# Two residual blocks in split fp32: the SBUF pools placed from both ends, TensorE's streamed operands low and its weights high

## The chip, the core and the metric

One NeuronCore of a Trainium2 chip runs the whole program in one launch. The metric is the device time of that launch in microseconds (us), the median of several runs; lower is better.

## What is computed

512 tokens of width 1024 go through two blocks, all in fp32. Each block is a SwiGLU feed-forward net (hidden width 2816), a mixer, and a second SwiGLU net, each with an RMS norm ahead and a residual around it:

```
h = h + 0.5 * ffn(rmsnorm(h), ffn1_w_in, ffn1_w_out)      # gate, up = x @ w_in; (silu(gate) * up) @ w_out
h = h + mixer(rmsnorm(h))                                  # block 1: retention + multiscale pool
                                                           # block 2: short conv + gated delta rule
h = h + 0.5 * ffn(rmsnorm(h), ffn2_w_in, ffn2_w_out)
return rmsnorm(h)
```

Some 203 MB of weights are read once; nearly all of the arithmetic is the matrix products.

## The kernel before

**Layout.** Activations lie transposed: 128 channels on the partitions, the 512 tokens along the free dimension. The residual is eight tiles h[k] of 128x512.

**Split products.** Full precision is had from one-pass matmuls (float32r) by splitting each operand: hi is the value rounded to what one pass takes (ScalarE), lo the rest (VectorE). `mm3` (L217 to L220) makes a product of three matmuls, each of 128x128 weights and 512 streamed columns, into one PSUM tile: wh with hi (L218), wh with lo (L219), wl with hi (L220). The first operand is loaded into the array (the *weights*), the second is *streamed* through it, four bytes for each column and partition.

**Weights.** `weights` (L208) loads one stage of 128x1024 fp32 by a DMA from SyncE into `wr` (three buffers), and splits it into `wh` and `wl` (three buffers each). All three tags lie in the pool `wts`.

**Streamed operands.** The rows of the residual, times a norm's gain, are split into sixteen tiles hi and lo of the pool `xsplit`; the first product of every net and mixer streams these. What comes after a first product is split into pools of its own that open and close with a stage: `act` (the 22 hidden rows of a net, for its second product), `att`, `ret`, `win`, `pool`, `mrg` in the first mixer, `ys` and others in the second. In the scores and in probabilities times values of the retention (pool `att`, lines L218 to L220 with the names psc and pso) both operands are such tiles; in the values themselves (L530 to L532) the roles are turned: the rows of `xsplit` are the weights, and `wh` and `wl` are streamed, 256 columns at a time. A norm's sums over partitions are two matmuls (L279) with the constant tile `onesr` as weights and two tiles `t` of the pool `tmp` streamed. In the second mixer L807 does what `mm3` does elsewhere, interleaved by a table with the steps of the delta rule; L722 multiplies a small tile `wbs` (16 columns of weights) with the rows of `xsplit`.

**Where pools lie.** Pools are laid in SBUF from low addresses up, in the order in which they are opened: const, hres, xsplit, wts, tmp, rows, and then those that open and close. [...]

## Time and profile before

| | us |
|---|---|
| median of 3 runs | 2308.33 (2307.97 to 2309.64) |
| the profiled execution, span from first to last instruction | 2307.3 |
| PE busy in it | 2272.6 (98%) |
| DVE busy | 1137.0 (49%) |
| ACT busy | 810.3 (35%) |
| DMA, mean rate | 90 GB/s |

The profiled execution is told by its span; the median of the runs stands 1.0 us above it. PE is TensorE's matmuls, PEld its weight loads, DVE VectorE, ACT ScalarE, POOL GpSimd. Matmuls are pipelined, so that the duration shown of one is longer than the time from its start to that of the next: what a matmul costs is read from the distance of starts in the timeline. L218 is line 218 of the kernel before.

### The profile page before, as it was taken

How to read it: one execution, taken by the hardware profiler on the slowest of the kernel's cores; microseconds unless marked ns; L12 is line 12 of the kernel's file. 1: busy time of each engine (PE TensorE's matmuls, PEld its weight loads, DVE VectorE, ACT ScalarE, POOL GpSimd, SP SyncE). 2: the span in 40 equal slices, each digit the busy share in tenths (PEclk: the TensorE clock that was granted, in tenths of full speed). 3: DMA queues.
4: the chain of work that ended last, by engine and by line, in shares of the span. 5: the costliest groups of instructions: out<-in, count | busy, mean ns of one | idle time of the engine just before them, and what ended most of it. 6: DMA issues, size and time to landing. Idle time of an engine off the chain costs nothing. (4 is left out here: it accounts for less than half of the span.)

```text
span 2307.3 us, 25697 instructions
## 1 busy us (share of the span) xinstructions
PE 2272.6 (98%) x10476; PEld 1863.1 (81%) x10476; DVE 1137.0 (49%) x1703; ACT 810.3 (35%) x1059; POOL 76.3 (3%) x78
## 2 busy tenths in 40 slices
PE   8999999999999999999999999999999999999998
PEld 6888888888878888888888888887777778888887
DVE  6444434665553444444336444334867655444332
ACT  5232223444432234233235332223534344233221
POOL 1000000000210000000000000000111000000000
PEclk9999999999999999999999999999999999999999
DMA  4333333222233333333333333333211123323332
GB/s 158 92 100 100 92 93 108 87 87 83 74 100 101 91 99 99 99 94 98 94 91 95 98 99 96 90 99 93 65 46 37 47 58 98 101 91 101 94 94 69
DMA packets 61190, 208.34 MB, mean 90 GB/s; under 512 B 6800, under 2 KB 9232, under 8 KB 61072
## 3 DMA queue, kind: packets, MB, share of 16 engines
q1 hardware_dynamic: 58544, 203.48, 28.9%
q10 hardware_dynamic: 2528, 3.21, 0.4%
q8 instruction: 82, 1.34, 0.2%
q14 instruction: 36, 0.29, 0.0%
HBM read 204.57 MB, written 2.10 MB: 90 GB/s over the span
## 5 line engine op out<-in xcount | busy, mean ns | idle before, releaser
L218 PE MATMUL ps<-hi,wh 128*128 128x512 f32 (+1 forms) x2774 | 1082.8, 391 | 6.4 <-ACT wh L202 6.4
L219 PE MATMUL ps<-lo,wh 128*128 128x512 f32 (+1 forms) x2774 | 1082.4, 390 | 0.8 <-DVE lo L206 0.8
L220 PE MATMUL ps<-hi,wl 128*128 128x512 f32 (+1 forms) x2774 | 1082.3, 390 | 0.6 <-DVE wl L203 0.6
L202 ACT ACTIVATE wh<-wr 128x1024 fp32r<-128x1024 f32 (+1 forms) x390 | 406.3, 1042 | 1159.6 <-PE ps L219 630.8
L203 DVE TENSOR_TENSOR wl<-wr,wh 128x1024 fp32r<-128x1024 f32 (+1 forms) x390 | 470.2, 1206 | 341.1 <-ACT wh L202 340.8
L218 PEld LDWEIGHTS ps<-hi,wh 128*128 128x128 f32 x2774 | 521.9, 188 | 119.5 <-ACT wh L202 6.4
L219 PEld LDWEIGHTS ps<-lo,wh 128*128 128x128 f32 x2774 | 521.5, 188 | 115.7 <-DVE lo L206 3.2
L220 PEld LDWEIGHTS ps<-hi,wl 128*128 128x128 f32 x2774 | 521.5, 188 | 114.9 <-DVE wl L203 2.5
L366 DVE TENSOR_TENSOR t<-ps,rb 128x512 f32<-128x512 f32 x88 | 60.7, 690 | 258.6 <-PE ps L220 258.6
L363 DVE TENSOR_TENSOR t<-ps,rb 128x512 f32<-128x512 f32 x88 | 60.8, 690 | 169.9 <-PE ps L220 169.8
L202 ACT ACTIVATE hi<-t 128x512 fp32r<-128x512 f32 x119 | 75.2, 632 | 112.2 <-DVE t L368 62.0
L807 PE MATMUL ps<-hi,wh 128*128 128x512 f32 x224 | 94.4, 422 | 0.4 <-DVE t L1001 0.4
L807 PE MATMUL ps<-hi,wl 128*128 128x512 f32 x224 | 93.3, 416 | 0.0
L807 PE MATMUL ps<-lo,wh 128*128 128x512 f32 x224 | 92.6, 413 | 0.0
L203 DVE TENSOR_TENSOR lo<-t,hi 128x512 fp32r<-128x512 f32 x119 | 83.3, 700 | 5.4 <-ACT hi L202 5.1
L368 DVE TENSOR_TENSOR t<-t,t 128x512 f32<-128x512 f32 x88 | 60.8, 691 | 8.2
L364 ACT ACTIVATE t<-t 128x512 f32<-128x512 f32 x88 | 54.2, 616 | 3.4 <-DVE t L363 3.3
L377 DVE SCALAR_TENSOR_TENSOR h<-ps,h 128x512 f32<-128x512 f32 x31 | 21.4, 691 | 64.4 <-PE ps L220 64.4
L807 PEld LDWEIGHTS ps<-hi,wh 128*128 128x128 f32 x224 | 42.9, 191 | 8.2 <-issue 1.0
L807 PEld LDWEIGHTS ps<-hi,wl 128*128 128x128 f32 x224 | 42.4, 189 | 8.3 <-issue 0.9
L807 PEld LDWEIGHTS ps<-lo,wh 128*128 128x128 f32 x224 | 43.1, 192 | 6.9 <-issue 0.2
L530 PE MATMUL pv<-wh,hi 128*128 128x256 f32 x128 | 36.3, 284 | 0.0
(292 smaller groups left out, 1362.1 us busy)
## 6 DMA issues: line engine op xcount, KB each, us to landing
wr<-in_ffn_w_in SPq DMA_DIRECT2D x176, 512.0 KB, 3.5
wr<-in_ffn_w_out SPq DMA_DIRECT2D x64, 512.0 KB, 3.6
wr<-in_w_in SPq DMA_DIRECT2D x48, 512.0 KB, 3.5
wr<-in_w_mix_in SPq DMA_DIRECT2D x28, 512.0 KB, 3.5
wr<-in_ffn_w_out SPq DMA_DIRECT2D x32, 384.0 KB, 3.1
wr<-in_w_v SPq DMA_DIRECT2D x8, 512.0 KB, 3.8
wr<-in_w_ret_up SPq DMA_DIRECT2D x8, 512.0 KB, 3.4
wr<-in_w_pool_up SPq DMA_DIRECT2D x8, 512.0 KB, 3.5
```

The costliest lines, as they stand in the source:

```text
L202: nc.scalar.activation(hi, src, AF.Copy)
L203: nc.vector.tensor_tensor(lo, src, hi.bitcast(F32), ALU.subtract)
L218: nc.tensor.matmul(ps, lh, rh, start=start, stop=False)
L219: nc.tensor.matmul(ps, lh, rl, start=False, stop=False)
L220: nc.tensor.matmul(ps, ll, rh, start=False, stop=stop)
L363: nc.vector.tensor_tensor(g, pg, rb, ALU.mult)
L364: nc.scalar.activation(g, g, AF.Silu)
L366: nc.vector.tensor_tensor(u, pu, rb, ALU.mult)
L368: nc.vector.tensor_tensor(m, g, u, ALU.mult)
L377: nc.vector.scalar_tensor_tensor(h[d], ps, 0.5, h[d], ALU.mult, ALU.add)
L530: nc.tensor.matmul(pv, xh[:, sl], wh[:, k % 4, :], start=(k == 0), stop=False)
L807: nc.tensor.matmul(ps, a[:, k, :], b, start=(k == j == 0), stop=(k == KD - 1 and j == 2))
```

## The change

Every SBUF pool is given a side. The side "right" lays a pool from the far end of SBUF down, the side "left" (the default) from address 0 up. `const`, `hres`, `wts`, `tmp` and `rows` go to the far end; `wh` and `wl` get a pool `wsplit` of their own there. `xsplit` and all pools that open and close with a stage stay on the left. The scratch area shrinks from 16384 to 1024 bytes. Comments and docstrings are blanked, and lines move by up to three.

```diff
+SCRATCH = 1024
...
-    def pool(self, ctx, name, psum=False):
-        kw = dict(space=bass.MemoryType.PSUM) if psum else {}
+    def pool(self, ctx, name, psum=False, far=False):
+
+        kw = dict(space=bass.MemoryType.PSUM) if psum else dict(side="right" if far else "left")
         return ctx.enter_context(self.tc.tile_pool(name=name, bufs=1, reuse_waits="tile", **kw))
...
-    const = K.pool(ctx, "const")
-    hp = K.pool(ctx, "hres")
+    const = K.pool(ctx, "const", far=True)
+    hp = K.pool(ctx, "hres", far=True)
     xp = K.pool(ctx, "xsplit")
-    wp = K.pool(ctx, "wts")
-    tp = K.pool(ctx, "tmp")
-    rp = K.pool(ctx, "rows")
+    wp = K.pool(ctx, "wts", far=True)
+    wsp = K.pool(ctx, "wsplit", far=True)
+    tp = K.pool(ctx, "tmp", far=True)
+    rp = K.pool(ctx, "rows", far=True)
...
-        wh = wp.tile([P, nk, m], F32R, name=nm("wh"), tag="wh", bufs=3)
-        wl = wp.tile([P, nk, m], F32R, name=nm("wl"), tag="wl", bufs=3)
+        wh = wsp.tile([P, nk, m], F32R, name=nm("wh"), tag="wh", bufs=3)
+        wl = wsp.tile([P, nk, m], F32R, name=nm("wl"), tag="wl", bufs=3)
...
-    nc = _bacc.Bacc("TRN2", target_bir_lowering=False, num_devices=1)
+    nc = _bacc.Bacc("TRN2", target_bir_lowering=False, num_devices=1, dynamic_dma_scratch_size=SCRATCH)
```

No instruction is added, removed or moved: both built programs have the same instructions, with the same waits, in the same order on every engine. What differs is where tiles lie. The table has the bytes within a partition at which they lie in the two built programs, and what is left of each start when it is divided by 64 (it is the same for every tile of a row, and for every slice of it that a matmul of 256 or 512 streamed columns takes, since these start at multiples of 512 bytes into their tile):

| tiles | before | mod 64 | after | mod 64 |
|---|---|---|---|---|
| hi, lo of `xsplit` | 34,976 to 67,743 | 32 | 1,152 to 33,919 | 0 |
| hi, lo of `act`, `att`, `ret`, `win`, `pool`, `mrg`, `ys` | 130,176 to 228,863 | 0 | 33,920 to 132,607 | 0 |
| `wh` | 80,032 to 92,319 | 32 | 174,016 to 186,303 | 0 |
| `wl` | 92,320 to 104,607 | 32 | 186,304 to 198,591 | 0 |
| `t` of `tmp` | 110,752 to 120,991 | 32 | 163,776 to 174,015 | 0 |
| `onesr` | 18,048 | 0 | 228,800 | 0 |
| `wbs` (starts 64 bytes apart) | 223,008 | 32 | 126,752 | 32 |
| h | 18,592 to 34,975 | 32 | 210,880 to 227,263 | 0 |

Matmuls of 512 streamed columns in float32r, counted in the built program before: 6048 stream `xsplit` against `wh` or `wl` (5376 by L218 to L220, 672 by L807); 2862 stream a stage's tiles against `wh` or `wl`; 48 have a stage's tiles on both sides; 22 are those of L279, 16 those of L722, 16 belong to the delta rule. Of 256 columns: 384 are the values of the retention (L530 to L532), 132 the last output row (L218 to L220, `act` against `wh` or `wl`), 48 the retention's scores and outputs.

## Rows read from the trace of the kernel before

**Rows 1.** The page: the span, the busy time of the engines, the granted clock of TensorE in 40 slices, and three of the costliest groups (busy us, mean ns of one | idle before them and what ended it); then the landing time of the largest group of loads.

```profile
span 2307.3 us, 25697 instructions
PE 2272.6 (98%) x10476; PEld 1863.1 (81%) x10476; DVE 1137.0 (49%) x1703; ACT 810.3 (35%) x1059; POOL 76.3 (3%) x78
...
PEclk9999999999999999999999999999999999999999
...
L218 PE MATMUL ps<-hi,wh 128*128 128x512 f32 (+1 forms) x2774 | 1082.8, 391 | 6.4 <-ACT wh L202 6.4
...
L202 ACT ACTIVATE wh<-wr 128x1024 fp32r<-128x1024 f32 (+1 forms) x390 | 406.3, 1042 | 1159.6 <-PE ps L219 630.8
L203 DVE TENSOR_TENSOR wl<-wr,wh 128x1024 fp32r<-128x1024 f32 (+1 forms) x390 | 470.2, 1206 | 341.1 <-ACT wh L202 340.8
...
wr<-in_ffn_w_in SPq DMA_DIRECT2D x176, 512.0 KB, 3.5
```

**Rows 2.** The waits of PE over the whole span, longest first in total (us in total, times, longest).

```profile
PE ps L218 <- ACT wh L202: 6.4, 1, 6.4
PE pg L918 <- DVE zu L928: 4.9, 2, 2.7
```

**Rows 3.** Busy time by stretch: from the start of the stretch to its end, its length, and the busy us and number of instructions of each engine, the granted clock, the DMA share and GB/s. The first stretch is the first product of the first net, the second the second product of block 2's first net.

```profile
35.20:252.20 217.00, 217.00 (x959) 179.73 (x958) 104.74 (x127) 72.71 (x89) 0.00 (x0) 1.00 0.32 96
...
1469.80:1592.80 123.00, 123.00 (x529) 99.03 (x528) 42.03 (x47) 33.05 (x39) 0.41 (x2) 1.00 0.32 92
```

**Rows 4.** Timeline of PE in the first product of a net (`xsplit` against `wh` and `wl`): start in us, duration, instruction. Between the third and the last row shown lie 21 more.

```profile
99.73 0.39 PE L218 MATMUL ps<-hi,wh 128*128 128x512 f32 x1
99.96 0.39 PE L219 MATMUL ps<-lo,wh 128*128 128x512 f32 x1
100.19 0.39 PE L220 MATMUL ps<-hi,wl 128*128 128x512 f32 x1
...
105.17 0.39 PE L218 MATMUL ps<-hi,wh 128*128 128x512 f32 x1
```

**Rows 5.** The same in the second product of a net (`act` against `wh` and `wl`), again with 21 rows between the third and the last.

```profile
1471.83 0.40 PE L218 MATMUL ps<-hi,wh 128*128 128x512 f32 x1
1472.06 0.40 PE L219 MATMUL ps<-lo,wh 128*128 128x512 f32 x1
1472.29 0.40 PE L220 MATMUL ps<-hi,wl 128*128 128x512 f32 x1
...
1477.43 0.40 PE L218 MATMUL ps<-hi,wh 128*128 128x512 f32 x1
```

**Rows 6.** Timeline of PE at the start of the retention's scores (both operands in `att`): the six matmuls of 512 columns, and the first of 384.

```profile
410.27 0.39 PE L218 MATMUL psc<-hi,hi 128*128 128x512 f32 x1
410.50 0.40 PE L219 MATMUL psc<-lo,hi 128*128 128x512 f32 x1
410.74 0.39 PE L220 MATMUL psc<-hi,lo 128*128 128x512 f32 x1
410.97 0.39 PE L218 MATMUL psc<-hi,hi 128*128 128x512 f32 x1
411.19 0.39 PE L219 MATMUL psc<-lo,hi 128*128 128x512 f32 x1
411.42 0.39 PE L220 MATMUL psc<-hi,lo 128*128 128x512 f32 x1
411.65 0.33 PE L218 MATMUL psc<-hi,hi 128*128 128x384 f32 x1
```

**Rows 7.** Timeline of PE around the two matmuls of a norm's sums (`t` against `onesr`; the two are shown as one row, x2), with `xsplit` against `wh` and `wl` before and after. Five rows are left out before the last.

```profile
439.29 0.39 PE L219 MATMUL ps<-lo,wh 128*128 128x512 f32 x1
439.51 0.40 PE L220 MATMUL ps<-hi,wl 128*128 128x512 f32 x1
439.75 0.63 PE L279 MATMUL pr<-t,onesr 128*128 128x512 f32 x2
440.22 0.40 PE L218 MATMUL ps<-hi,wh 128*128 128x512 f32 x1
...
441.60 0.39 PE L218 MATMUL ps<-hi,wh 128*128 128x512 f32 x1
```

**Rows 8.** Timeline of PE: the second and the sixteenth of the 16 matmuls of L722 (`xsplit` against the 16 columns of `wbs`), 14 apart.

```profile
1598.30 0.39 PE L722 MATMUL pba<-lo,wbs 128*16 128x512 f32 x1
...
1601.52 0.39 PE L722 MATMUL pba<-lo,wbs 128*16 128x512 f32 x1
```

**Rows 9.** Timeline of PE, matmuls of 256 columns: two of the retention's values, 9 apart.

```profile
398.99 0.28 PE L532 MATMUL pv<-wh,lo 128*128 128x256 f32 x1
...
400.07 0.28 PE L532 MATMUL pv<-wh,lo 128*128 128x256 f32 x1
```

**Rows 10.** The same for the last output row (`act` against `wh` and `wl`): two that are 15 apart.

```profile
2293.68 0.28 PE L220 MATMUL ps<-hi,wl 128*128 128x256 f32 x1
...
2295.45 0.28 PE L220 MATMUL ps<-hi,wl 128*128 128x256 f32 x1
```

**Rows 11.** The page's groups of two VectorE operations of one shape, one that writes tiles `t`, one that reads and writes h.

```profile
L366 DVE TENSOR_TENSOR t<-ps,rb 128x512 f32<-128x512 f32 x88 | 60.7, 690 | 258.6 <-PE ps L220 258.6
...
L377 DVE SCALAR_TENSOR_TENSOR h<-ps,h 128x512 f32<-128x512 f32 x31 | 21.4, 691 | 64.4 <-PE ps L220 64.4
```

## The prediction

> **What bounds the kernel now.** I read the page first, then the waits of PE, then stretches, then single matmuls. In the page [rows 1] PE is busy for 2272.6 of 2307.3 us at the full clock, DVE for 49% and ACT for 35%: TensorE is the bound. Its waits [rows 2] are small: 6.4 us for the first weights, then 4.9 us in the delta rule. In the products, which are most of the span, PE is busy without a gap [rows 3]: 217.00 of 217.00 us in a first product, 123.00 of 123.00 us in a second. A change that moves no instruction and no wait can only matter there by what one matmul costs. Durations don't tell that, since matmuls overlap; distances of starts do.

> In a first product 24 matmuls take 105.17 - 99.73 = 5.44 us, 226.7 ns each [rows 4]. In a second product, with the same shape, type, clock and weights buffers, 24 take 1477.43 - 1471.83 = 5.60 us, 233.3 ns each [rows 5]. [...] Nothing waits in either [rows 3], so this is a price inside TensorE's reading, and what differs between the two is where the streamed tile lies: `xsplit` in the one, `act` in the other.

> **Which property of the place?** Three readings are open, and the other rows choose between them.

> - *A high streamed tile is slow.* Against it: in the scores both operands are tiles of `att`, at 130,176 bytes or above, and after three matmuls the distances are 410.97 to 411.19 to 411.42 to 411.65, 0.22 to 0.23 us each [rows 6], the cheap price.
> - *Streamed tile and weights in different halves are slow.* The scores (both high) and the first products (both low) fit, and the second products (one high, one low) fit. The norm's sums do not fit well: there both distances together are 440.22 - 439.75 = 0.47 us, 0.235 each [rows 7], the dear price, with `onesr` at 18,048 and `t` at 110,752 and up. `wl` reaches to 104,607 and is still near to `xsplit`, so the border would have to lie between 104,608 and 110,752, which is neither half of anything in the table.
> - *Starts that differ modulo 64 bytes are slow.* By the table, first products have 32 and 32, scores 0 and 0: cheap. Second products have 0 streamed against 32, the norm's sums 32 against 0: dear. [...]

> I take the third. The change then makes every large pair equal: after it `xsplit`, the stage tiles, `wh`, `wl`, `t` and `onesr` all start at 0 modulo 64.

> **The sum.** Against the profiled execution's 2307.3 us:

> - Second products and their like: 2862 matmuls of 512 columns stream a stage's tiles against `wh` or `wl`. From 233.3 to 226.7 ns [rows 5, 4], 2862 x 6.67 ns = 19.1 us less. All of it lies on PE's path, since PE has no gap there [rows 3]. Would the loads hold? A stage of weights is used up in 24 matmuls, 5.44 instead of 5.60 us; its landing takes 3.5 us and its split 1.04 and 1.21 us [rows 1], three stages deep, and DVE is busy for 42.03 of 123.00 us [rows 3]. They do; were the cover gone, DVE's split of the next stage would be late first.
> - First products: 6048 matmuls, already cheap: 0.
> - The norm's sums: from 439.51 to 441.60 are nine distances [rows 7], 2.09 us where 9 x 226.7 ns make 2.04: 0.05 us of detour and return, eleven times: 0.5 us less.
> - 256 columns: the retention's values (32 against 32) take 1.08 us for 9, 120.0 ns each [rows 9]; the last output row (0 against 32) 1.77 us for 15, 118.0 ns [rows 10]. So the last row's 132 may go to 120.0 (0.3 us more), or the 384 values to 118.0 (0.8 us less). I take the first, since they then have equal starts as the values do; the bounds are -0.8 and +0.3.
> - VectorE and ScalarE: the same operations on tiles that lie elsewhere. Of one shape, VectorE takes 690 ns where it writes `t`, 691 where it works on h [rows 11], tiles 90,000 bytes apart: 0.
> - DMAs: none added or moved, the same order on SP's queue; the smaller scratch is one that no DMA here uses: 0.

> Together 19.1 + 0.5 - 0.3 = 19.3 us less, a span of 2288.0 us. The median of the runs stands 1.0 us above the span before, so I predict **2289 us**. A reading of starts is good to 0.01 us in 24 matmuls, at either price: 2862 x 0.8 ns = 2.4 us at most. With the values' 0.8 us and a run-to-run spread of 1.7 us this case reaches from 2284 to 2294.

> **What speaks against it.** [...] And the 16 matmuls of L722, 32 against 32, never settle at 226.7: 1601.52 - 1598.30 = 3.22 us for 14, 230.0 each [rows 8]. They have 16 columns of weights and not 128, which may excuse them.

> **The rivals.**

> - *Halves.* If a pair in different halves is dear, the change makes all of them so: weights lie at 174,016 and up, everything streamed against them below 132,608. The 2862 stay at 233.3, the 6048 go there: 6048 x 6.67 = 40.3 us more, **2348 us**, slower. It decides if the price hangs on the distance between weights and stream; L722, with weights at 223,008 and dearer than 226.7 [rows 8], speaks for it, the norm's sums and the odd border against it. 0.15.
> - *A finer rule of starts.* In rows 4 and 6 the starts agree modulo 512, not only 64; after the change they differ by 320 (174,016 less 1,152 is 337 x 512 + 320). If that counts, the nearest row is L722, whose starts differ by multiples of 64: 230.0 ns [rows 8] for all 8910 matmuls. 6048 x 3.3 = 20.0 us more, 2862 x 3.3 = 9.4 less: **2319 us**. For it: only L722 shows such pairs, and it doesn't settle. [...] 0.12.
> - *The streamed tile's place alone*, or its place as against weights that lie lower: the scores speak against the first, and nothing against the second, which halves don't need to be symmetrical for. The 2862 become cheap and the 6048 stay so: 19.1 us less, **2289 us** as well, for another reason. 0.10.
> - *The place does nothing*, and the second product is dearer for a reason of its own, such as its 66 matmuls into one PSUM tile as against 24: **2308 us**. Against it: the norm's sums, two matmuls into a tile, are dear as well [rows 7]. 0.08.

> [...]

> **How the numbers follow.** My case has 0.55. The bound of telling from no change is 0.2%, 4.6 us. Faster: 0.55 + 0.10 = 0.65. Same: 0.08. Slower: 0.15 + 0.12 = 0.27. The likeliest case's own range is 2284 to 2294. The range for 8 in 10 takes in the case of no effect and the finer rule with the same 2.4 us of reading, 2284 to 2322; left out are the halves.

> **What would show it.** Right: in a second product 24 matmuls in 5.44 us, a stretch of 528 matmuls in about 119.7 instead of 123.2 us, the two of a norm's sums 0.45 us apart from start to the next product, the first products still at 5.44 us, PE still without gaps. Wrong: first products at 5.60 us (halves), or at 5.5 with an uneven pattern (finer rule); or second products still at 5.60 (no effect of place). [...]

## The result

The changed kernel takes **2341.78 us** (median of 4 runs, 2340.92 to 2342.66) where the kernel before takes 2308.98 on the same chip (2307.97 to 2309.80): a ratio of 1.0142, with a 95% interval of 1.0128 to 1.0156. It is slower by 32.8 us. The prediction said 2289, with a range that ended at 2322.

In the page of the changed kernel, the answers to [rows 1]:

```profile
span 2339.1 us, 25697 instructions
PE 2305.0 (99%) x10476; PEld 1858.6 (79%) x10476; DVE 1138.0 (49%) x1703; ACT 810.1 (35%) x1059; POOL 76.0 (3%) x78
...
PEclk9999999999999999999999999999999999999999
...
L221 PE MATMUL ps<-hi,wh 128*128 128x512 f32 (+1 forms) x2774 | 1092.2, 394 | 6.4 <-ACT wh L205 6.4
...
L206 DVE TENSOR_TENSOR wl<-wr,wh 128x1024 fp32r<-128x1024 f32 (+1 forms) x390 | 470.5, 1207 | 341.4 <-ACT wh L205 341.1
```

The span grew by 31.8 us and PE's busy time by 32.4. The clock, the counts and the other engines are as before: VectorE's split of a stage takes 1207 ns (1206 before). All of the loss is in TensorE's own pace.

The stretches that answer to [rows 3], the first product of the first net and the second product of block 2's first net (it begins 25.4 us later now):

```profile
35.20:252.20 217.00, 217.00 (x932) 173.93 (x931) 102.77 (x125) 71.60 (x87) 0.00 (x0) 1.00 0.29 92
...
1495.20:1618.20 123.00, 123.00 (x529) 99.11 (x528) 42.09 (x47) 33.08 (x39) 0.41 (x2) 1.00 0.31 92
```

PE has no gap in either. In the same 217 us the first product gets through 932 matmuls instead of 959; the second product is at its 529 as before.

The timeline of PE, places that answer to [rows 4, 9, 7, 5, 10] in this order. In the first product and in the second the two rows are 24 matmuls apart; the values' two (L535) 9 apart; then the norm's sums and the next product; the last row's two 15 apart.

```profile
100.03 0.39 PE L221 MATMUL ps<-hi,wh 128*128 128x512 f32 x1
...
105.62 0.39 PE L221 MATMUL ps<-hi,wh 128*128 128x512 f32 x1
...
406.45 0.28 PE L535 MATMUL pv<-wh,lo 128*128 128x256 f32 x1
...
407.51 0.28 PE L535 MATMUL pv<-wh,lo 128*128 128x256 f32 x1
...
447.57 0.62 PE L282 MATMUL pr<-t,onesr 128*128 128x512 f32 x2
448.03 0.39 PE L221 MATMUL ps<-hi,wh 128*128 128x512 f32 x1
...
1490.25 0.40 PE L221 MATMUL ps<-hi,wh 128*128 128x512 f32 x1
...
1495.85 0.40 PE L221 MATMUL ps<-hi,wh 128*128 128x512 f32 x1
...
2325.41 0.28 PE L223 MATMUL ps<-hi,wl 128*128 128x256 f32 x1
...
2327.18 0.28 PE L223 MATMUL ps<-hi,wl 128*128 128x256 f32 x1
```

24 matmuls of a first product take 105.62 - 100.03 = 5.59 us, 233 ns each: they went from the cheap price to the dear one. 24 of a second product take 5.60 us, the dear price, as before. So nothing became cheap, and what was cheap is lost. The values became cheaper, 1.06 us for 9, 117.8 ns against 120.0. The last fifteen of the last row stay at 1.77 us, 118.0 each, but the greater part of that row became cheaper. Two of its matmuls 24 apart, in the kernel before and in the changed one:

```profile
2279.91 0.28 PE L220 MATMUL ps<-hi,wl 128*128 128x256 f32 x1
...
2282.75 0.28 PE L220 MATMUL ps<-hi,wl 128*128 128x256 f32 x1
```

```profile
2312.14 0.28 PE L223 MATMUL ps<-hi,wl 128*128 128x256 f32 x1
...
2314.86 0.28 PE L223 MATMUL ps<-hi,wl 128*128 128x256 f32 x1
```

That is 2.84 us against 2.72, 118.3 ns each against 113.3. Why the last fifteen differ from these was not traced.

The small product that answers to [rows 8], L725 now, two matmuls 14 apart again:

```profile
1623.72 0.40 PE L725 MATMUL pba<-lo,wbs 128*16 128x512 f32 x1
...
1626.93 0.39 PE L725 MATMUL pba<-lo,wbs 128*16 128x512 f32 x1
```

It takes 3.21 us, 229.3 ns each, where it took 230.0.

**Where the 31.8 us lie.** By the first starts of each stage in the two traces, the first products of the four nets went from 246.10, 239.67, 240.46 and 239.67 us to 253.00, 246.62, 247.09 and 246.62: 27.4 us. The first mixer took 4.9 us more, the second 0.1 less, the second products of the nets nothing (122.96 and 122.97 for the first net's), the tail after the last of them, with the last row, 0.5 less. Sum: 31.7.

### The profile page after: what moved, and what is told of

Its sections match the earlier page's. It is cut to its first block, busy times and chain, and to the rows that moved or that the text cites. A ratio compares the mean times of both kernels' runs of the same rounds, so it can differ in the third digit from the quotient of the medians.

```text
span 2339.1 us, 25697 instructions
## 1 busy us (share of the span) xinstructions
PE 2305.0 (99%) x10476; PEld 1858.6 (79%) x10476; DVE 1138.0 (49%) x1703; ACT 810.1 (35%) x1059; POOL 76.0 (3%) x78
## 3 DMA queue, kind: packets, MB, share of 16 engines
q10 hardware_dynamic: 2528, 3.21, 0.5%
## 5 line engine op out<-in xcount | busy, mean ns | idle before, releaser
L206 DVE TENSOR_TENSOR wl<-wr,wh 128x1024 fp32r<-128x1024 f32 (+1 forms) x390 | 470.5, 1207 | 341.4 <-ACT wh L205 341.1
```

The source lines that it names most:

```text
L206: nc.vector.tensor_tensor(lo, src, hi.bitcast(F32), ALU.subtract)
```

## The experiments

How prices are read here: a stretch counts every matmul that reaches into it, two more than it has distances. 100 us at 226.7 ns hold 441 and show x443; at 233.3 they hold 429 and show x430 or x431. One count is 0.5 ns. Below, a **difference** is the streamed tile's start less that of its weights, modulo 512 or, later, 256; counted so, the changed kernel has 1,152 - 174,016 = -338 x 512 + 192, a difference of 192 (the 320 of the prediction is the same, counted from the weights). The pads are tiles that nothing uses. Each kernel here but the last was run once. The kernel before took 2309.25 us beside the first four, 2309.62 beside the one with differences of 32 to 8, and 2309.43 beside the others.

Three readings were to be told apart first: that different *halves* are dear; that starts must be *alike modulo 512*, the finer rule; and that the place itself counts, both starts at 32 modulo 64 being cheap.

**The kernel before with every tile 32 bytes higher.**

```diff
+    const.tile([P, 8], F32, name="pad")
     vec = const.tile(...)
```

> The kernel before with a pad of 32 bytes per partition ahead of everything: all tiles move up by 32 bytes, so xsplit and the weights both start at 0 modulo 64 (192 modulo 512), and the stage tiles at 32 (160 modulo 512). Halves (streamed tile and weights on different sides of a border are dear): nothing changes, first products 226.7 ns a matmul, second products 233.3, 2309 us. Equal starts modulo 512 (dear unless streamed tile and weights start alike): the same, 2309 us, since first products still agree and second ones still differ by 32. [...]

Measured: 2309.75 us. The stretches of net 1's first product and net 3's second product:

```profile
100.00:200.00 100.00, 100.00 (x443) 82.78 (x442) 46.65 (x56) 30.54 (x37) 0.00 (x0) 1.00 0.31 96
1470.00:1570.00 100.00, 100.00 (x430) 80.48 (x430) 35.37 (x40) 27.66 (x33) 0.00 (x0) 1.00 0.31 91
```

Nothing moved: first products cheap, second products dear. First products now start at 0 modulo 64, which by the third reading makes them dear, and second products stream from 32, so the residue itself doesn't count; what counts depends on the pair.

**The kernel before with the weights 320 bytes higher.** All stays low, only the difference of first products changes, from 0 to 192.

```diff
+    wp.tile([P, 80], F32, name="pad")
     vec = const.tile(...)
```

> The kernel before with a pad of 320 bytes at the start of the weights' pool: weights and all that lies above them move up by 320 bytes, xsplit stays. Streamed tile and weights of the first products then differ by 320 modulo 512, as they do after the change, with both still in the low half. Halves: first products stay at 226.7 ns, 2309 us. Equal starts modulo 512: first products go to 233.3 ns, about 2342 us. Both at 32 modulo 64: xsplit is at 32 and the weights too (480 modulo 512), so 226.7 ns and 2309 us.

Measured: 2341.56 us, the time of the change.

```profile
100.00:200.00 100.00, 100.00 (x430) 80.17 (x429) 45.04 (x54) 29.45 (x36) 0.00 (x0) 1.00 0.30 95
1470.00:1570.00 100.00, 100.00 (x430) 80.52 (x429) 35.84 (x41) 27.01 (x32) 0.00 (x0) 1.00 0.32 92
```

All of the loss is here without any pool at the far end. The halves are refuted as its cause.

**The changed kernel with the streamed side 320 bytes higher.** The halves stay apart, the difference becomes 0.

```diff
+    xp.tile([P, 80], F32, name="pad")
     vec = const.tile(...)
```

> The changed kernel with a pad of 320 bytes ahead of xsplit: everything on the left side moves up by 320 bytes, so that xsplit, the stage tiles and the weights all start alike modulo 512 (448), with weights still in the high half and all streamed tiles in the low one. Halves: nothing changes, first and second products 233.3 ns, 2342 us. Equal starts modulo 512: both go to 226.7 ns, about 2289 us. Both at 32 modulo 64: all are at 0, so 2342 us.

Measured: 2290.0 us, span 2288.2.

```profile
100.00:200.00 100.00, 100.00 (x443) 82.77 (x442) 46.86 (x57) 30.66 (x38) 0.00 (x0) 1.00 0.30 95
1470.00:1570.00 100.00, 100.00 (x443) 82.81 (x442) 35.51 (x40) 28.77 (x35) 0.00 (x0) 1.00 0.33 98
```

320 bytes turn the change from 33 us slower than before to 19 us faster, and both products are cheap.

**The kernel before with only the stages' tiles 32 bytes higher.** The counterpart with everything low: second products get a difference of 0.

```diff
+    rp.tile([P, 8], F32, name="pad")
     vec = const.tile(...)
```

> The kernel before with a pad of 32 bytes at the start of the pool rows: the stage tiles move up by 32 bytes, xsplit and weights stay. All then start alike modulo 512 (160) and at 32 modulo 64, with the stage tiles still high and the weights low. Halves: nothing changes, second products 233.3 ns, 2309 us. Equal starts modulo 512: second products go to 226.7 ns, about 2289 us. Both at 32 modulo 64: the same, 2289 us.

Measured: 2291.12 us.

```profile
100.00:200.00 100.00, 100.00 (x443) 82.81 (x442) 46.69 (x57) 30.57 (x37) 0.00 (x0) 1.00 0.31 95
1470.00:1570.00 100.00, 100.00 (x443) 82.79 (x442) 35.51 (x40) 28.45 (x34) 0.00 (x0) 1.00 0.34 101
```

Both are cheap again. So equal starts are cheap wherever the two tiles lie; 64 is not enough to agree in, 512 is. The next two ask in what they must agree, with four differences each.

**Differences of 64, 128, 192 and 256.** The kernel just told, with a pad of its own at the start of `act` in each net.

```diff
+    act_pads = [64, 128, 192, 256]
...
             ap = K.pool(c, nm("act"))
+            ap.tile([P, act_pads.pop(0) // 4], F32, name=nm("pad"))
```

> Stage tiles start at 160 modulo 512 as xsplit, wh and wl do, but the pool act of the four nets begins 64, 128, 192 and 256 bytes later in turn, so that the second products of the four nets (528, 528, 528 and 462 matmuls of 512 columns) have starts that differ by 64, 128, 192 and 256 modulo 512. All else has equal starts. The same kernel without these pads took 2291.1 us. Starts must agree modulo 512: all four second products at 233.3 ns a matmul (24 in 5.60 us), 2046 x 6.67 ns = 13.6 us more, about 2305. Modulo 256: the last net's is cheap (24 in 5.44 us), 1584 x 6.67 = 10.6 us more, about 2302. Modulo 128: those of nets 2 and 4 are cheap, 1056 x 6.67 = 7.0 us more, about 2298. A price that grows with the difference: four different distances, between 226.7 and 233.3.

Measured: 2299.42 us. The second products of the four nets in order (the last stretch is 70 us long):

```profile
270.00:370.00 100.00, 100.00 (x439) 82.05 (x438) 33.57 (x38) 26.88 (x33) 0.00 (x0) 1.00 0.34 98
1110.00:1210.00 100.00, 100.00 (x430) 80.42 (x430) 38.03 (x45) 32.61 (x41) 0.00 (x0) 1.00 0.32 94
1470.00:1570.00 100.00, 100.00 (x430) 80.14 (x429) 33.81 (x37) 26.50 (x32) 0.00 (x0) 1.00 0.32 92
2185.00:2255.00 70.00, 70.00 (x311) 57.96 (x310) 21.43 (x23) 19.99 (x23) 0.00 (x0) 1.00 0.32 95
```

256 apart is cheap (70 us / 309 = 226.5 ns): it is modulo 256 that starts must agree, not 512. 128 and 192 are dear (100 / 428 = 233.6). 64 has a price of its own that no theory had: 100 / 437 = 228.8. With these, 528 x 2.1 + 1056 x 6.67 ns = 8.2 us, and 2291.1 + 8.2 = 2299.3 is the time measured. That it fits to 0.1 us is partly luck: outside these products PE waits 1.6 us for the weights `wbs` in the second mixer, where it waited 0.2 in the kernel before, and the first mixer is 1.2 us shorter than in the kernel just told.

**Differences of 320, 384, 448 and 96.**

```diff
-    act_pads = [64, 128, 192, 256]
+    act_pads = [320, 384, 448, 96]
```

> The same with 320, 384, 448 and 96 bytes in place of 64, 128, 192 and 256. Modulo 512 or 256: all four second products at 233.3 ns, 2046 x 6.67 = 13.6 us more than 2291.1, about 2305. Modulo 128: the second net's (384) is cheap, 1518 x 6.67 = 10.1 us more, about 2301. A price that grows with the distance around the circle of 512 bytes would give 448 the price of 64 and 384 that of 128. 96 is the difference in the second products of the kernel before and should give its 233.3 ns under every theory.

Measured: 2304.76 us.

```profile
270.00:370.00 100.00, 100.00 (x439) 82.05 (x438) 33.73 (x38) 26.94 (x33) 0.00 (x0) 1.00 0.34 98
1110.00:1210.00 100.00, 100.00 (x430) 80.45 (x429) 37.85 (x45) 32.44 (x41) 0.00 (x0) 1.00 0.32 95
1470.00:1570.00 100.00, 100.00 (x430) 80.17 (x429) 33.81 (x37) 26.75 (x32) 0.00 (x0) 1.00 0.32 92
2185.00:2255.00 70.00, 70.00 (x302) 56.31 (x301) 19.84 (x21) 19.33 (x24) 0.00 (x0) 1.00 0.33 96
```

320, 384 and 448 repeat 64, 128 and 192 to the count, as a period of 256 has it. 448 is dear and 64 nearly cheap, so the price isn't the distance around the circle: a stream that starts 64 bytes after its weights' residue pays little (100 / 437 = 228.8 ns), one that starts 64 bytes before it pays in full (100 / 428 = 233.6). The difference of 96 is dear, as expected, but it is not that of the second products of the kernel before, as the expectation has it: theirs is -32, or 224. The time is 2.4 us above the sum of these prices (528 x 2.1 + 1518 x 6.67 = 11.2 us). That excess is not in the products but in the second mixer. There PE waits 2.35 us for `wbs`, and from 1594.00 to 1598.00 us the granted clock is 0.57 of full speed in the mean, and 14 of L725's distances take 4.77 us, where the changed kernel has a clock of 1.00 and 3.21 us. The two are worth more than the 2.4 us; the first mixer is 1.2 us shorter than in the kernel without pads.

```profile
1594.19 0.49 PE L725 MATMUL pba<-hi,wbs 128*16 128x512 f32 x1 [2.35 <-DVE wbs L205]
...
1594.00:1598.00 4.00, 3.81 (x10) 1.38 (x11) 0.14 (x1) 1.18 (x1) 0.00 (x0) 0.57 0.00 0
```

**64 bytes between `wh` and `wl`.** Does each matmul pay for its own pair?

```diff
+    pads = []
...
+        if not pads:
+            pads.append(wp.tile([P, 16], F32, name="padl"))
         wl = wp.tile([P, nk, m], F32R, name=nm("wl"), tag="wl", bufs=3)
```

> 64 bytes lie between wh and wl, so that a matmul with weights wl starts 64 bytes off its streamed tile in the first products while the two with wh start alike (2016 of 6048 differ); the stage tiles move by 64 too, so that in the second products wl agrees and wh doesn't (1908 of 2862 differ). The kernel without this took 2291.1 us. If each matmul pays for its own pair of starts, 24 of a first product take 16 x 226.7 + 8 x 233.3 ns = 5.49 us and 24 of a second 8 x 226.7 + 16 x 233.3 = 5.55 us: 2016 x 6.67 + 1908 x 6.67 = 26.2 us more, about 2317. If a change from one state to the other is what is paid for, once each way, or if a difference anywhere makes the whole sequence dear: 5.60 us in both, (6048 + 2862) x 6.67 = 59.4 us more, about 2350. If a price falls only on a matmul that follows one with other starts, first products pay 2 of 3 and second 2 of 3 as well: about 2331.

Measured: 2318.61 us. Net 1's first product and net 3's second:

```profile
100.00:200.00 100.00, 100.00 (x434) 81.30 (x433) 45.34 (x54) 29.47 (x36) 0.00 (x0) 1.00 0.32 95
1470.00:1570.00 100.00, 100.00 (x438) 81.96 (x437) 35.64 (x40) 26.88 (x32) 0.00 (x0) 1.00 0.32 93
```

The time fits the first expectation, and the rows do not, so that it fits by chance. In the first products one matmul in three has a difference of 192, the others 0. Own prices would give (2 x 226.7 + 233.3) / 3 = 228.9 ns and x439. The count is 434, 100 / 432 = 231.5 (231.1 by the first and last start of 930 of them): as much as if two of three were dear, which is what the third expectation says of first products. But the extra time isn't spread as it says: in the mean the step from the start of the one dear matmul (L224) to the next takes 235.8 ns, the other two 228.3 and 229.2. In the second products two of three have 64 and one 0, and the count is 438 where all three at 64 had 439. So the price belongs to the sequence and not to the matmul alone; a lone dear pair between cheap ones cost about twice its price here, 3 x 4.4 = 13.3 ns for 6.7.

**Differences of 32, 160, 16 and 8.** On the kernel with all starts alike; for the last two the tiles of `act` are 256 bytes longer and used from 16 or 8 bytes on.

```diff
+    act_pads = [32, 160, 16, 8]
...
+            pad = act_pads.pop(0) // 4
+            if pad >= 8:
+                ap.tile([P, pad], F32, name=nm("pad"))
+                pad = 0
...
-                acts.append(split(ap, "a", 2 * KF, m))
+                acts.append(split(ap, "a", 2 * KF, m, [P, T + 64] if pad else None, off=pad))
```

> As in the two runs with the pool act moved, but the second products of the four nets differ in their starts by 32, 160, 16 and 8 bytes (in the last two the tiles are 256 bytes longer and used from 16 or 8 bytes on; the scratch area has 1024 bytes to make room, which moves everything by 30 x 512). Known by now, modulo 256: 0 gives 226.7 ns a matmul, 64 gives 228.9, 96, 128, 192 and 224 give 233.3. If the price is one of the difference modulo 256 in steps of 64 bytes, 8, 16 and 32 lie in the step of 0 and cost 226.7 to 228.9, 160 costs 233.3: 528 x 6.67 = 3.5 us more than the 2291.1 us of equal starts, up to 3.5 us more for the others: 2294.6 to 2298. If any difference that isn't a multiple of 64 is dear, whatever its size: 233.3 for all four, 2046 x 6.67 = 13.6 us more, 2305.

Measured: 2303.41 us.

```profile
270.00:370.00 100.00, 100.00 (x430) 80.30 (x430) 33.88 (x39) 26.71 (x32) 0.00 (x0) 1.00 0.32 93
1110.00:1210.00 100.00, 100.00 (x428) 80.39 (x427) 35.59 (x41) 30.03 (x37) 0.00 (x0) 1.00 0.32 93
1470.00:1570.00 100.00, 100.00 (x434) 81.15 (x433) 32.83 (x37) 27.11 (x32) 0.00 (x0) 1.00 0.32 95
2185.00:2255.00 70.00, 70.00 (x302) 56.57 (x301) 19.84 (x21) 19.28 (x23) 0.00 (x0) 1.00 0.32 95
```

32 and 8 are dear, 16 nearly (100 / 432 = 231.5), 160 a shade more than dear (100 / 426 = 234.7). Steps of 64 are refuted: 8 bytes cost what 128 cost (70 / 300 = 233.3 ns here, 100 / 428 = 233.6 for 128 above). (PE waits 1.6 us for `wbs` in this kernel too.)

**The version that beats both.** The changed kernel with the pad of 320 bytes, and one of 128 in the pool `win`, whose tiles were the last pairs to differ.

```diff
+    xp.tile([P, 80], F32, name="pad")
     vec = const.tile(...)
...
                 pp = K.pool(c2, nm("win"))
+                pp.tile([P, 32], F32, name="padw")
```

> The changed kernel with 320 bytes more at the start of the pool xsplit, and 128 more in the pool win, so that every pair of streamed tile and weights starts alike modulo 512 while the halves stay apart. With the first pad alone it took 2290.0 us. Equal starts decide: 226.7 ns for all 8910 matmuls, about 2289 us, 19 to 20 us below the kernel before and 52 below the change. If the halves cost anything of their own, it stays above the 2291.1 us of the same starts with everything low; if not, they agree within 0.1%.

Measured: 2290.98 us (4 runs, 2288.98 to 2292.46), a ratio to the kernel before of 0.9916, interval 0.9900 to 0.9933. It is 18.5 us faster than before, and 51 us faster than the change. The same starts with everything low took 2291.12: the two ends of SBUF are worth nothing that these runs can tell. Its timeline of the last output row, two matmuls 15 apart, beside the changed kernel's 1.77 us:

```profile
2277.53 0.28 PE L224 MATMUL ps<-hi,wl 128*128 128x256 f32 x1
...
2279.33 0.28 PE L224 MATMUL ps<-hi,wl 128*128 128x256 f32 x1
```

1.80 us, 120.0 ns each: with 256 columns equal starts are dearer than the changed kernel's 118.0 and 113.3. The difference of 96 (the last net in the run with 320, 384, 448 and 96) is no cheaper than equal starts there, 2.88 us for 24, 120.0 each.

## Why the prediction was wrong, step by step

- **What bounds the kernel: right.** In the products PE is without gaps before and after, no other engine's time moved (VectorE 1138.0 us busy, 1137.0 before; ScalarE 810.1 and 810.3), and the change acts through the distance of two matmuls' starts alone.
- **That pairs with equal starts cost 226.7 ns and others 233.3: right** for most differences (64 bytes cost 228.9), and so was the sum for a kernel in which all are equal. It gave a span of 2288.0; the run with 320 bytes added has 2288.2, and second products at x443. The loads kept up. That the spans agree to 0.2 us is luck: the last version, with nearly the same starts, has times from 2288.98 to 2292.46.
- **"The change then makes every large pair equal": this step failed.** I compared starts modulo 64, and they must agree modulo 256. After the change they differ by 192. Every cheap row of before [rows 4, 6] agreed modulo 512 and every dear one [rows 5, 7] differed by 32 modulo 64, so 64, 128, 256 and 512 all fitted, and the sum rested on one of four. Taking 64 of the four was my own estimate, which no row and no run shows, and the runs refute it: by the prices found below, differences of 8, 128 and 192 bytes cost 6.6 ns more than equal starts, 64 bytes 2.2.
- **The finer rule was right in kind and wrong in size.** I priced it with L722 at 230.0 ns [rows 8], which gave 2319. For one difference of 192 the price is the dear one, 233.3, on first products, and the second products gain nothing. L722 was no price for this rival at all. Its weights start 64 bytes apart in turn, so before the change its matmuls run through the differences 128, 64, 0 and 192, and (226.7 + 228.9 + 2 x 233.3) / 4 = 230.5 seems to fit. After the change they run through 96, 32, 224 and 160, which by the prices found below would make 233.6, and the same 14 distances take 3.21 us, 229.3 each. With 16 columns of weights the price does not follow the differences. So [rows 8] told nothing of multiples of 64, the reserve about its 16 columns was sound, and no row of before could part 64 from 256.
- **The cost of 6048 first products** was counted at 40.3 us for the halves; at that price it came to 32.3 in the nets and mixers. The four nets' 4224 took 27.4 (6.5 ns each). The 672 of the second mixer, which I had put down as if they were all on PE's path, took nothing. That PE waits for the delta rule there anyway would explain it, but is not shown: PE stands idle for 15.5 us of the mixer before and 15.3 after. The first mixer took 4.9 more with the values' gain of 0.8 in it, where its 1152 were due 7.7; the rest was not traced.
- **The halves, the streamed tile's place, no effect of place:** refuted by the two runs with 320 bytes, which give the loss with everything low and the gain with the halves apart.
- **256 columns: the other way round.** I took the last row to go to 120.0. With equal starts both kinds cost 120.0. In the change the values go to 117.8 (a difference of 64) and gain 384 x 2.2 ns = 0.8 us, which was one of the two bounds; most of the last row goes from 118.3 (224) to 113.3 (192).
- **The norm's sums:** their own starts are alike now (163,776 and 228,800, both 192 modulo 256), and to the next product it is 0.46 us instead of 0.47, with dear neighbours on both sides. The term was 0.5 us and decides nothing.
- **The DMAs' 0:** no run shows what the scratch area is used by. In the changed kernel every DMA is issued on the queues of SyncE and ScalarE, as before, the largest group of loads lands in 3.5 us, as before, and PE has no gap in the products.

## What to carry to other kernels

Where long runs of such matmuls (float32r, 128x128 weights, 512 columns) each load new weights and PE has no gaps, look at the starts of the streamed tile and of the weights modulo 256 before judging a new layout; here a pad of 320 bytes was worth 52 us of 2342, and what the layout was meant to do was worth nothing. When a rule is inferred from a few rows, list every rule that fits them and look for the row that parts them; where there is none, as here, the rows prefer none of them, and only a run can tell. A total that fits an expectation says less than the rows of each stage.

## What the runs showed of the hardware

| difference in bytes | 0 | 8 | 16 | 32 | 64 | 96 | 128 | 160 | 192 | 224 |
|---|---|---|---|---|---|---|---|---|---|---|
| ns | 226.7 | 233.3 | 231.7 | 233.3 | 228.9 | 233.3 | 233.3 | 234.3 | 233.3 | 233.3 |

Each is worked out from the first and last start of 440 to 990 matmuls of one stage in the trace (224 are the second products of before); the stretches and timelines shown agree to 0.5 ns. The differences from 8 to 160 were each seen in one net of one run (64 and 128 in two). Not expected were the period of 256, that 64 is nearly cheap where 192 is not, and that one dear pair among two cheap ones costs twice its price. The table doesn't hold for other shapes: with 16 columns of weights the small product takes 230.0 and 229.3 with two quite different sets of differences, and with 256 streamed columns equal starts are among the dearest, 120.0 against 113.3 to 118.3.

The weights of the next matmul are loaded while one streams. In the kernel before the load for L220's matmul, which starts at 1000.21 us, takes 0.19 us from 999.98 on, where L219's matmul starts:

```profile
999.98 0.39 PE L219 MATMUL ps<-lo,wh 128*128 128x512 f32 x1
1000.21 0.39 PE L220 MATMUL ps<-hi,wl 128*128 128x512 f32 x1
...
999.98 0.19 PEld L220 LDWEIGHTS ps<-hi,wl 128*128 128x128 f32 x1
```

No run here shows why the period is 256 bytes, nor whether the weights that count are a matmul's own or the next one's; this stays open, as does the price of a mixed sequence.
